# Keys, group-0 values and bias tables of a dilated attention layer sent through DRAM instead of through TensorE

## The chip, the cores and the metric

The kernel runs on one core of a Trainium2 chip. The metric is the device time of one execution in microseconds (us). Five engines share the work: TensorE (PE in the profile, with PEld for its weight loads), VectorE (DVE), ScalarE (ACT), GpSimd (POOL) and SyncE (SP), which here only issues DMAs. Each engine works off its own list of instructions strictly in order, so an instruction that waits holds up everything behind it on its engine.

## The reference, cut to what matters

Two encoder layers over 512 tokens of width 1024, 16 heads of 64 columns, all in float32. Layer A is a dilated attention: one projection gives, for each of three groups (dilations 1, 4, 16), a query, a key and a value, and a gate.

```python
for g, (window, dilation) in enumerate(((128, 1), (512, 4), (2048, 16))):
    q = rms_norm(qkv[:, :, g, 0], q_gain[g])      # per head, over 64 columns
    k = rms_norm(qkv[:, :, g, 1], k_gain[g])
    v = qkv[:, :, g, 2]
    logits = q @ k.T * scale + bias[t5_bucket(rel * dilation)]   # |rel| <= reach, else -1e30
    o, lse = softmax(logits) @ v, log-denominator
y = sum_g softmax_g(lse) * o                       # the three groups merged
x = x + (y * silu(gate)) @ w_out
```

Layer B is a two-dimensional neighbourhood attention of the same size; the change does not touch its code, only the tile that its raw queries and keys live in.

## The kernel before

**Tiling.** Layer A goes through eight chunks `hc`, each of two heads (128 columns). A chunk has these projections on PE: `rawk` (keys of groups 1 and 2, and their values `v12`), `rawq` (queries of the three groups and the key of group 0), `v0_a` (value of group 0, computed transposed) and `gate_a`. Float32 is split into a high and a low part (`wh`, `wl` for the weights, `hn_h`, `hn_l` for the tokens), and three matmuls make one product (`mm3`). Weights come in 512 KB loads `wraw` (three buffers), ACT casts `wh`, and DVE or POOL subtracts for `wl` (four buffers each).

**Order.** PE's order is written out by hand: `main()` yields the projections, `side()` the attention of the chunk before, and `run` slips pieces of the one between pieces of the other by a running estimate of PE's time (`clock`). `later_on(delay, job)` places a job at such a time. On ACT, DVE, POOL and SP the compiler's scheduler chooses the order, except where `tc.keep_in_program_order` holds it. All DMAs but one go through SP's queue.

**Queries and keys.** Scores need queries and keys with the 64 head columns on the partitions, the projection gives tokens on the partitions. In chunks 0 to 5 (`moved(hc)`) the queries and group 0's key are turned without PE: DVE transposes 32x32 blocks in place (`turn_q`, L574), SP writes the tile to DRAM (`qd<-rawq`, L613) and reads it back in another order (`qt<-qd`, L619), and ACT scales group 0's key into `k0` (`split_q`, L638 with L652). The keys of groups 1 and 2 go through PE: `k_a` makes eight 128x128 transposes in each chunk (`transpose4`, L219), DVE scales them into `k12` (L566). The value of group 0 is turned by four PE transposes in `v_a`, and ACT copies them into `v0` (L647). The attention of chunk `hc` runs while PE projects chunk `hc + 1`: `rawk` of `hc + 1`, then `weigh` of chunk `hc - 1` (`PE o`), then the scores of chunk `hc` (`PE log`) between matmuls of `rawq`. Probabilities already go through DRAM as well (`td<-tr`, L764, and `pt<-td`, L768).

**Bias.** `bias_lines` multiplies a one-hot table with the bias table on PE (`pl`), subtracts from a mask on DVE and writes short lines to DRAM. `bias_a` reads them for each chunk into `e0` and `e12` with six loads (`e<-l_d`, L714, L721) whose rows overlap: the source pattern steps back by one row for each partition, and its outermost dimension counts 4.

Of the kernel before, what the change touches and what calls it, by code (L numbers as in the profile page):

```python
# [46 lines left out]
def tile_hybrid_encoder(  # L47
# [6 lines left out]
    t5t: bass.AP,  # L54
    rpb: bass.AP,
    onehot: bass.AP,
# [39 lines left out]
    l0_d = dr.tile([16, 4, 400], F32, name="l0_d")  # L96
    l12_d = dr.tile([16, 512], F32, name="l12_d")
# [186 lines left out]
    def squares(v, ss, i, ns):  # L284
        sq = wk.tile([P, 512], F32, tag="sq", name="sq")[:, : ns * 64]
        if len(v.shape) == 3:
            v = v.rearrange("p (a f) r -> p a f r", f=4)
            nc.gpsimd.tensor_mul(sq.rearrange("p (f a r) -> p a f r", f=4, a=4), v, v)
# [8 lines left out]
    def head_norm(raw, ss, ns, held, delay=0, quick=False):  # L297
# [5 lines left out]
        def scale():  # L303
            for i in range(4):
                by = rs[:, i * ns : (i + 1) * ns].unsqueeze(2)
                if len(raw.shape) == 4:
                    v = raw[:, :, i, :].rearrange("p (h a f) r -> p f h a r", h=2, f=4)
                    by = rs[:, i * ns : (i + 1) * ns].rearrange("p (f h) -> p f h", h=2)
                    by = by.unsqueeze(3).unsqueeze(4).to_broadcast([P, 4, 2, 2, 32])
# [4 lines left out]
                if held or delay:  # L314
                    tc.keep_in_program_order(m)

# [98 lines left out]
    def bias_lines():  # L415

        oh = wk.tile([32, 896], F32, tag="rawq", name="oh", bufs=1)
        tc.keep_in_program_order(nc.sync.dma_start(oh, onehot))
        t5 = cp.tile([32, 48], F32, name="t5")
        nc.sync.dma_start(t5, t5t)  # L420
# [23 lines left out]
    rk = wk.tile([P, 4608], F32, tag="rawk", name="rawk", bufs=1)  # L444
# [6 lines left out]
    def project_qk(n, ns, key, hc, guard, first=False, **kw):  # L451

        box = []

        def evac(i, acc):
            if not box:
                if key == "rawq":
                    t = wk.tile([P, 4 * n], F32, tag="rawq", name=key, bufs=1)
                    box.append(
                        t.rearrange("p (c i r) -> p c i r", c=16, i=4)  # L460
                        if moved(hc)
                        else t.rearrange("p (i c) -> p i c", i=4)
                    )
                elif key == "rawk":
                    box.append(part(0))
                    st["v12", hc] = part(1 + hc % 3)
                elif key == "v":
                    box.append(rk[:, 4 * n * hc : 4 * n * hc + 4 * n].rearrange("p (i c) -> p i c", i=4))
                else:
                    t = wk.tile([P, 4 * n], F32, tag="rawq", name=key, bufs=1)  # L470
                    box.append(t.rearrange("p (i c) -> p i c", i=4))
                box.append(None if key == "v" else wk.tile([P, 32], F32, tag="ss", name="ss"))
            raw, ss = box
            if key == "rawq" and moved(hc):
                src = acc.rearrange("p (f a r) -> p f a r", f=4, a=4)
                pieces = [(raw[:, :, i, :].rearrange("p (a f) r -> p f a r", a=4), src)]
            elif key == "rawk":
                pieces = [(raw[:, i, :], acc[:, :256]), (st["v12", hc][:, i, :], acc[:, 256:])]
            else:
                pieces = [(raw[:, i, :], acc[:, :n])]  # L480
# [5 lines left out]
            if not first and key != "v":  # L486
                squares(raw[:, :, i, :] if key == "rawq" and moved(hc) else raw[:, i, : ns * 64], ss, i, ns)
# [843 lines left out]
```

## Time and profile before

| | |
|---|---|
| time, median of 3 runs | 842.3 us (841.99 to 843.98) |
| the profiled execution: its own time, its span | 842.18 us, 840.4 us |
| PE busy / DVE / ACT / POOL | 833.6 / 515.4 / 425.1 / 283.5 us |
| granted TensorE clock | 1.000 |
| DMA | 141.25 MB, mean 168 GB/s; SP's queue q1 holds 54.6% of 16 engines' span |

The span runs from the first to the last instruction; 1.8 us of the profiled time lie outside it. In rows of the timeline the columns are start, duration, engine, line, operation, output and input tiles, count, and in brackets the idle time before it and what ended it. A matmul's duration (0.39 us) overlaps with the next; the distance of starts (0.227 us) is what PE's time is made of.

### The profile page before, as it was taken

To read this page: it belongs to the slowest core of one execution; us is meant where nothing else is said; L and a number is where in the kernel's file an instruction comes from. 1 tells how busy PE (TensorE), PEld (TensorE's weight loads), DVE (VectorE), ACT (ScalarE), POOL (GpSimd) and SP (SyncE) were. 2 spreads that over 40 slices of the span, in tenths; PEclk is the share of its full clock that TensorE was granted. 3 is DMA by queue.
4 is the path that set the end of the run, shared out by engine and by line. 5 is a ranking of instruction groups with operands and counts; after the bars stand their busy time and mean duration, and the time that the engine had idled before them with its cause. 6 is when DMAs were issued, how large, how long until landed. Compare 5 with 4: busy or idle time off the path is not lost.

```text
span 840.4 us, 15567 instructions
## 1 busy us (share of the span) xinstructions
PE 833.6 (99%) x5698; PEld 675.0 (80%) x5698; DVE 515.4 (61%) x1355; ACT 425.1 (51%) x893; POOL 283.5 (34%) x432
## 2 busy tenths in 40 slices
PE   9999999999999999999999999999999999999998
PEld 7788888788788788788788787888878877777787
DVE  7355684684584675575574755548456778668653
ACT  7432653553552652652653564345375465663551
POOL 3352442441441432432531341112521625235211
PEclk9999999999999999999999999999999999999999
DMA  7346468478368478387376364165236646457223
GB/s 254 112 122 189 150 194 245 164 215 260 127 186 238 143 222 245 107 228 231 111 221 184 111 195 126 56 231 183 78 98 182 180 142 182 129 151 204 102 94 132
DMA packets 64221, 141.25 MB, mean 168 GB/s; under 512 B 5648, under 2 KB 23248, under 8 KB 64144
## 3 DMA queue, kind: packets, MB, share of 16 engines
q1 hardware_dynamic: 64000, 139.99, 54.6%
q8 instruction: 45, 0.74, 0.4%
q14 instruction: 32, 0.26, 0.1%
q10 hardware_dynamic: 144, 0.26, 0.1%
HBM read 109.11 MB, written 31.12 MB: 167 GB/s over the span
## 4 chain that ended last, share of the span: by engine, by line
PE 93%; ACT 3%; DVE 2%; issue 1%; DMA 1%; POOL 0%; SPq 0%; DVEq 0%; ACTq 0%
PE acc L215 79%; PE o L215 5%; PE log L215 5%; PE tp L219 3%; ACT p L1101 1%; ACT p L679 1%; DVE hn_l L403 1%; DMA wraw<-in_w 1%; ACT wh L132 0%; DVE raw L313 0%; DVE p L1091 0%; ACT raw L485 0%; DVE pt L999 0%; DVE wl L138 0%; PE pa L215 0%
## 5 line engine op out<-in xcount | busy, mean ns | idle before, releaser
L132 ACT CAST wh<-wraw 128x512 fp32r<-128x512 f32 (+1 forms) x259 | 158.4, 613 | 288.8 <-PE acc L215 236.7
L215 PE MATMUL acc<-wh,hn_h 128*128 128x512 f32 x704 | 281.9, 401 | 1.3 <-ACT hn_h L402 0.7
L215 PE MATMUL acc<-wl,hn_h 128*128 128x512 f32 x704 | 274.1, 390 | 0.3 <-POOL wl L138 0.3
L215 PE MATMUL acc<-wh,hn_l 128*128 128x512 f32 x704 | 274.3, 390 | 0.0
L138 POOL TENSOR_TENSOR wl<-wraw,wh 128x512 fp32r<-128x512 f32 (+1 forms) x104 | 135.5, 1302 | 362.6 <-ACT wh L132 337.9
L138 DVE TENSOR_TENSOR wl<-wraw,wh 128x512 fp32r<-128x512 f32 (+1 forms) x156 | 114.2, 732 | 148.7 <-ACT wh L132 148.0
L215 PEld LDWEIGHTS acc<-wh,hn_h 128*128 128x128 f32 x704 | 132.1, 188 | 35.5 <-issue 5.6
L215 PEld LDWEIGHTS acc<-wh,hn_l 128*128 128x128 f32 x704 | 132.1, 188 | 28.6
L215 PEld LDWEIGHTS acc<-wl,hn_h 128*128 128x128 f32 x704 | 132.4, 188 | 25.9 <-POOL wl L138 0.8
L215 PE MATMUL acc<-y,wh 128*128 128x512 f32 (+1 forms) x272 | 82.4, 386 | 0.0
L215 PE MATMUL acc<-hn_h,wh 128*128 128x512 f32 x192 | 76.1, 397 | 0.8 <-ACT rawk L485 0.6
L215 PE MATMUL acc<-hn_h,wl 128*128 128x512 f32 x192 | 74.9, 390 | 0.0
L215 PE MATMUL acc<-hn_l,wh 128*128 128x512 f32 x192 | 74.8, 390 | 0.0
L679 ACT ACTIVATE p<-p,mn 128x512 f32<-128x512 f32 (+3 forms) x128 | 69.3, 585 | 0.7 <-DVE mn L678 0.2
L291 DVE TENSOR_REDUCE ss<-sq 128x4 f32<-128x256 f32 (+1 forms) x96 | 48.5, 505 | 28.1 <-POOL sq L290 18.3
L839 ACT ACTIVATE p<-p,mn 128x512 f32<-128x512 f32 (+1 forms) x64 | 44.9, 702 | 38.5 <-DVE mn L828 38.5
L755 DVE STREAM_TRANSPOSE tr<-p 128x512 f32<-128x512 f32 (+1 forms) x80 | 53.6, 684 | 9.3 <-ACT p L679 8.7
L215 PEld LDWEIGHTS acc<-y,wh 128*128 128x128 f32 x272 | 48.3, 189 | 9.6 <-issue 1.3
L215 PE MATMUL acc<-y,wl 128*128 128x512 f32 (+1 forms) x136 | 51.5, 379 | 0.0
L215 PEld LDWEIGHTS acc<-hn_h,wh 128*128 128x128 f32 x192 | 36.0, 188 | 9.2 <-ACT rawk L485 1.0
L215 PEld LDWEIGHTS acc<-hn_h,wl 128*128 128x128 f32 x192 | 36.0, 188 | 7.7
L215 PEld LDWEIGHTS acc<-hn_l,wh 128*128 128x128 f32 x192 | 36.1, 188 | 7.1
(128 smaller groups left out, 965.6 us busy)
## 6 DMA issues: line engine op xcount, KB each, us to landing
wraw<-in_w SPq DMA_DIRECT2D x119, 512.0 KB
td<-tr SPq DMA_DIRECT2D x14, 1024.0 KB
pt<-td SPq DMA_DIRECT2D x56, 256.0 KB
qd<-rawq SPq DMA_DIRECT2D x6, 1024.0 KB
qt<-qd SPq DMA_DIRECT2D x24, 256.0 KB
td<-tr SPq DMA_DIRECT2D x6, 896.0 KB
pt<-td SPq DMA_DIRECT2D x24, 224.0 KB
e<-l_d SPq DMA_DIRECT2D x32, 112.0 KB
```

Source lines behind the costliest of these rows:

```text
L132: nc.scalar.copy(h, raw)
L138: eng.tensor_sub(l, raw, h.bitcast(F32))
L215: nc.tensor.matmul(o, l, r, **kw)
L219: nc.tensor.transpose(o, i, ident)
L291: nc.vector.tensor_reduce(ss[:, i * ns : (i + 1) * ns], sq.rearrange("p (a b) -> p a b", b=64), axis=AX.X, op=ALU.add)
L403: return nc.vector.scalar_tensor_tensor(l, xk, g, h.bitcast(F32), op0=ALU.mult, op1=ALU.subtract)
L679: nc.scalar.activation(pr, pr, AF.Copy, scale=mn[:, 3:4])
L755: nc.vector.transpose(dst, src[:, :n].rearrange("p (i b k) -> p i b k", b=4, k=32))
L839: nc.scalar.activation(row, row, AF.Exp, bias=mn[:, 1:2], scale=-1.0, accum_out=mn[:, 2:3])
L1101: nc.scalar.activation(pr[:, o : o + n], pr[:, o : o + n], AF.Exp, bias=mn[:, 0:1], scale=-1.0, accum_out=mn[:, 2:3])
```

## The change

In chunks 0 to 5 the keys of groups 1 and 2 no longer pass through PE. They are evacuated into the same tile as the queries (`rq`, 3072 columns in place of 2048; blocks 4 and 5 of each group of six), turned there by DVE (`turn_raw`), written and read together with the queries (rows of 768 elements, 1.5 MB in place of 1 MB each way), and scaled in place by ACT after they land. Scores read them from `qt`. In chunks 0 to 6 group 0's value is turned by one DVE transpose, a 256 KB write and four 64 KB reads, and ACT's copy into `v0` reads the result. The bias lines are subtracted once from a table that is now laid out on the host, written to DRAM (`line_d`), and copied by six DMAs from DRAM to DRAM into shifted rows; a chunk's bias then takes one load of 128 rows and four of 32. The raw key and value tile `rk` shrinks by 512 columns, since keys left it.

```diff
     def head_norm(raw, ss, ns, held, delay=0, quick=False, then=None):
...
+            if then:
+                then()
...
-        for g, (o, n) in enumerate(((0, 384), (384, 256), (640, 256))):
-            pl = bank("pl")
-            matmul(pl[0:16, :n], t5[:, 16 * g : 16 * g + 16], oh[:, o : o + n], start=True, stop=True)
-            nc.vector.tensor_sub(mk[:, o : o + n], mk[:, o : o + n], pl[0:16, :n])
-        for j in range(4):
-            nc.sync.dma_start(l0_d[:, j, j : j + 384], mk[:, 0:384])
-        nc.sync.dma_start(l12_d, mk[:, 384:896])
+        nc.vector.tensor_sub(mk, mk, t5)
+        nc.sync.dma_start(line_d, mk)
...
+        jobs = [(l0_d[:, 32 * j : 32 * j + 32, :], shifted(127 - j, 4, 256)) for j in range(4)]
+        jobs += [(l12_d[:, :, 224 * g : 224 * g + 224], shifted(384 + 256 * g + 31, 1, 224)) for g in range(2)]
+        for n, job in enumerate(jobs):
+            later_on(3000 + 2500 * n, partial(spread_out, *job))
...
     def normed(raw, ss, ns, key, hc):
-        head_norm(raw, ss, ns, False, 9000 if key == "rawk" and 0 < hc < NHC - 1 else 0)
-        if key == "rawq" and moved(hc):
-            turn_q(raw)
+        delay = (31000 if moved(hc) else 9000) if key == "rawk" and 0 < hc < NHC - 1 else 0
+        head_norm(raw, ss, ns, False, delay, then=partial(turn_raw, key) if moved(hc) else None)
...
+    def turn_raw(key):
+        f0, f1 = FS[key]
+        for a in range(0, 4, 2):
+            x = by_a[:, a : a + 2, P * f0 : P * f1]
+            tc.keep_in_program_order(nc.vector.transpose(x, x))
...
-        vt = wk.tile([P, EXT], F32, tag="vt", name="vt", bufs=1)
-        nc.vector.tensor_mul(trj(vt[:, 64:EXT]), to_trj(acc[0]), trj(rs_trj))
-        nc.gpsimd.tensor_copy(vt[:, 0:64], vt[:, EXT - 64 : EXT])
+        vt = wk.tile([P, S], F32, tag="vt", name="vt", bufs=1)
+        rows = lambda t, a, b: t.rearrange("p (s j) -> p s j", j=4)[:, a:b]
+        for a, b, to in ((0, 112, 16), (112, P, 0)):
+            src = to_trj(acc[0])[:, a:b]
+            nc.vector.tensor_mul(rows(vt, to, to + b - a), src, rows(rs_trj, a, b))
+        if hc < NHC - 1:
+            move_v(hc, vt)
...
+    def move_v(hc, vt):
+        d = dr.tile([4, P, P], F32, name="vd", tag="vd", bufs=2)
+        vx = wk.tile([P, 4, 4, 32], F32, tag="vx", name="vx", bufs=1)
+        nc.vector.transpose(vx.rearrange("p b i r -> p i b r"), vt.rearrange("p (i b r) -> p i b r", i=4, b=4))
...
+        later_on(2500, write)
+        for b in (0, 2, 1, 3):
+            later_on(7000, partial(read, b))
+        later_on(12500, place)
...
-            project_qk(512, 4, "rawk", hc, ("k12", hc - 1), first=hc == 0, need=None if hc else "na"),
+            project_qk(512, 4, "rawk", hc, ("k12" if hc == NHC - 1 else "q", hc - 1), first=hc == 0, need=None if hc else "na"),
...
     def k_a(hc):
-        yield "wait", ("rawk", hc), 12500 if hc == 0 else 22500 if hc < NHC - 1 else 10500
+        if moved(hc):
+            return
...
         def write():
-            src = raw.rearrange("p (a f) i r -> p a (f i r)", f=4)
-            tc.keep_in_program_order(nc.sync.dma_start(d.rearrange("a p x -> p a x"), src))
+            tc.keep_in_program_order(nc.sync.dma_start(d.rearrange("a p x -> p a x"), by_a))
...
         tc.keep_in_program_order(scaled(dst, src, 0))
+        for g in range(2):
+            x = qt[:, :, 4 + g, :]
+            tc.keep_in_program_order(scaled(x, x, g + 1))
...
     def v_a(hc):
+        if hc < NHC - 1:
+            return
...
+        load(e0, l0_d[hs].rearrange("h p c -> p h c"))
+        for j in range(4):
+            dst = e12[32 * j : 32 * j + 32].rearrange("p (h g) c -> p h (g c)", h=2)
+            load(dst, l12_d[hs].rearrange("h r c -> r h c"))
...
-                    (1 + g, j, slice(256 + P * g, 384 + P * g), k12[:, g, :], slice(P * j, P * j + P))
+                    (1 + g, j, slice(256 + P * g, 384 + P * g), qt[:, :, 4 + g, 32 * j : 32 * j + 32])
```

The order on SP shifts in every chunk. This is SP's queue before, from the second probability write of one chunk to the query reads of the next (`td`, `pt`: probabilities; `qd`, `qt`: queries; `wraw`: weights):

```order
L764 DMA td<-tr 128x4x512
L768 DMA pt<-td 32x4x512 x2
L184 DMA wraw<-in_w 128x1024 x2
L768 DMA pt<-td 32x4x512 x2
L184 DMA wraw<-in_w 128x1024 x2
L613 DMA qd<-rawq 128x4x512
L184 DMA wraw<-in_w 128x1024
L619 DMA qt<-qd 32x4x512 x4
```

The same place after the change, from the probability write to the query write (`vx`, `vd`, `vt`: group 0's value; `e`: bias):

```order
L803 DMA td<-tr 128x4x512
L184 DMA wraw<-in_w 128x1024 x2
L807 DMA pt<-td 32x4x512
L574 DMA vd<-vx 128x4x128
L760 DMA e_2698<-l_d 128x2x256
L760 DMA e_2699<-l_d 32x2x448 x4
L807 DMA pt<-td 32x4x512
L578 DMA vt<-vd 32x4x128 x4
L807 DMA pt<-td 32x4x512
L184 DMA wraw<-in_w 128x1024
L807 DMA pt<-td 32x4x512
```

Two weight loads moved ahead of the first probability read, and ten small DMAs (value and bias) came in behind it. Before, the bias loads of this chunk stood ahead of the `td` write.

On DVE, in the same stretch, before: from the scaling of the keys that PE turned to the start of the queries' norm (`ss`: sums of squares, `nv`: the norm).

```order
L566 TENSOR_SCALAR k_3272<-tp,gk 128x512
L755 STREAM_TRANSPOSE tr<-p 128x4x4x32 x2
L566 TENSOR_SCALAR k_3272<-tp,gk 128x512
L138 TENSOR_TENSOR wl<-wraw,wh 128x512
L291 TENSOR_REDUCE ss<-sq 128x8 x3
```

After, the same place, up to the turn of group 0's value:

```order
L794 STREAM_TRANSPOSE tr<-p 128x4x4x32 x2
L138 TENSOR_TENSOR wl<-wraw,wh 128x512
L290 TENSOR_REDUCE ss<-sq 128x8 x3
L138 TENSOR_TENSOR wl<-wraw,wh 128x512
L313 TENSOR_TENSOR rawq<-rawq,rs 128x2x4x32 x4
L290 TENSOR_REDUCE ss<-sq 128x8
L561 TENSOR_TENSOR vt<-acc,rs_trj 128x448
L561 TENSOR_TENSOR vt<-acc,rs_trj 128x64
L530 STREAM_TRANSPOSE rawq<-rawq 128x2x256 x2
L138 TENSOR_TENSOR wl<-wraw,wh 128x512
L112 TENSOR_SCALAR nv<-ss 128x32
L571 STREAM_TRANSPOSE vx<-vt 128x4x4x32
```

The two key scalings from PE's output are gone; the norm of the keys (four multiplications), their turn and the value's turn now stand here, ahead of the queries' norm.

More of the change, by code (lines that the diff above doesn't have):

```diff
@@ L560, in k_a @@
     def k_a(hc):
-        yield "wait", ("rawk", hc), 12500 if hc == 0 else 22500 if hc < NHC - 1 else 10500
-        k12 = wk.tile([P, 2, 512], F32, tag="k12", name="k12", bufs=1)
+        if moved(hc):
+            return
+        yield "wait", ("rawk", hc), 22500 if hc < NHC - 1 else 10500
+        qt = q_tiles(hc)[0]
         raw = st.pop(("rawk", hc))
@@ L628, in land @@
             assert not left[0]
[L629 to L630 removed]
+            split_q(qt, k0)
             yield
@@ L794, in scores @@
                 ]
-                for g, j, cols, keys, of in parts:
+                for g, j, cols, keys in parts:
                     for hd in range(2):
```

167 lines of the change are left out of this document (84 added, 83 removed).

## Prediction

> **What bounds the kernel now.** I read the page first, then who waits for whom, then the chain in order of time. The page:
>
> ```profile
> span 840.4 us, 15567 instructions
> PE 833.6 (99%) x5698; PEld 675.0 (80%) x5698; DVE 515.4 (61%) x1355; ACT 425.1 (51%) x893; POOL 283.5 (34%) x432
> PE 93%; ACT 3%; DVE 2%; issue 1%; DMA 1%; POOL 0%; SPq 0%; DVEq 0%; ACTq 0%
> ```
>
> PE is busy for 99% of the span and 93% of the chain that ended last is its own. The list of PE's waits begins with:
>
> ```profile
> PE busy L377 <- DVE warm L366: 0.9, 1, 0.9
> PE acc L215 <- ACT hn_h L402: 0.7, 1, 0.7
> ```
>
> Nothing made PE wait longer than 0.9 us, and both rows belong to the start or to the change of layers. So in layer A a PE instruction that goes away shortens the span, as long as nothing becomes late enough to make PE wait. The chain around the attention of chunk 4, and its one piece with `pl`:
>
> ```profile
> 300.29 0.44 PE tp L219 x4
> 302.12 0.44 PE tp L219 x4
> 325.73 0.44 PE tp L219 x4
> 341.18 3.62 PE o L215 x48
> 346.39 1.84 PE log L215 x96
> 36.82 1.61 PE pl L215 x6
> ```
>
> Four transposes hold the chain for 0.44 us (two groups for the keys, one for the value), and the one-hot products for 1.61 us.
>
> **What goes.** Chunks 0 to 5 lose two groups each, chunks 0 to 6 one: 12 + 7 = 19 groups, 19 x 0.44 = 8.4 us. The products with the one-hot table go once: 1.6 us. Together 10.0 us, all on the path. How one transpose reads by itself:
>
> ```profile
> L219 PE MATMUL tp<-ident,rawk 128*128 128x128 f32 x64 | 9.6, 272 | 0.0
> L215 PE MATMUL o<-pt,rawk 128*64 128x128 f32 x320 | 22.4, 278 | 0.0
> ```
>
> 272 ns is its duration with the overlap; a quarter of 0.44 us, 110 ns, is what it adds. The Trainium skill (TensorE: Matmul & The Clock Gate, Part 4: PE-mode transpose) gives about 275 ns for one in a kernel: by that the 76 transposes would be worth an estimated 20.9 us, against 8.4 us by the chain. The durations agree, but as a price the measured distance decides.
>
> The scores now read those keys in runs of 32 columns out of `qt`. The second row has a moving operand in runs of 32 too and takes 278 ns against 272, so I add nothing (bound: 6 ns on 8 chunks x 4 tiles x 2 groups x 4 residues x 2 heads = 512 matmuls, 3.1 us if none of it overlapped).
>
> **What is added off PE, and its cover.** The long new chain is: turn on DVE, write `qd`, read `qt`, scale on ACT, scores. Here it is for chunk 3 and chunk 4, from the timelines of SP, ACT and PE:
>
> ```profile
> 264.68 0.43 SPq L613 DMA_DIRECT2D qd<-rawq  x1
> 271.34 1.75 SPq L619 DMA_DIRECT2D qt<-qd  x4
> 273.22 3.03 ACT L485 ACTIVATE rawk<-acc,rs_n 128x256 f32<-128x256 f32 x8
> 277.77 1.20 ACT L652 ACTIVATE k<-qt,gk 128x512 f32<-128x512 f32 x1 [1.02 <-DMA qt<-qd]
> 282.40 1.86 PE L215 MATMUL log<-k,qt 64*32 64x192 f32 x93
> ...
> 322.11 1.29 DVE L574 STREAM_TRANSPOSE rawq<-rawq 128x512 f32<-128x512 f32 x2
> 325.10 0.43 SPq L613 DMA_DIRECT2D qd<-rawq  x1
> 332.35 1.75 SPq L619 DMA_DIRECT2D qt<-qd  x4
> 337.14 3.03 ACT L485 ACTIVATE rawk<-acc,rs_n 128x256 f32<-128x256 f32 x8
> 340.51 1.29 ACT L652 ACTIVATE k<-qt,gk 128x512 f32<-128x512 f32 x1
> ```
>
> In chunk 3 ACT waited for the read, which landed 277.77 - 271.34 = 6.4 us after its issue; in chunk 4 it did not wait. With 6.4 us there too, the read landed at 338.8, and the scaling could have ended 346.39 - 338.8 - 1.29 = 6.3 us ahead of the scores. That is the cover. Against it stand:
>
> ```profile
> 336.00:338.00 2.00, 2.00 (x10) 1.65 (x9) 0.69 (x1) 1.48 (x4) 0.31 (x1) 1.00 1.08 249
> 357.00:359.00 2.00, 2.00 (x62) 1.45 (x68) 0.94 (x3) 0.00 (x0) 0.00 (x0) 1.00 1.02 395
> L679 ACT ACTIVATE p<-p,mn 128x512 f32<-128x512 f32 (+3 forms) x128 | 69.3, 585 | 0.7 <-DVE mn L678 0.2
> ```
>
> The last two columns of the stretches are the busy share of 16 DMA engines and GB/s. While a write like `qd` and a weight load run, 395 GB/s move; while query reads and a weight load run, 249. So the write's extra 0.5 MB costs 1.3 us and the read's 2.1 us (at the least nothing, if rows of 3 KB in place of 2 KB carry it; at the most half of the whole, 3.6 us of the write's 7.25 and 3.2 us of the read's 6.4). I take the rates, since these stretches run full. Two more scalings on ACT: 1.2 us. The scores come 0.44 us earlier, by the value's transposes. Sum 5.0 of 6.3 us: 1.3 us are left.
>
> DVE comes in ahead of it. Its new work in front of the queries' turn:
>
> ```profile
> L313 DVE TENSOR_TENSOR rawk<-rawk,rs x32: 382/415/1489, 46.6 to 505.5; 128x256 f32<-128x256 f32 x32
> L574 DVE STREAM_TRANSPOSE rawq<-rawq x24: 662/699/705, 66.6 to 386.7; 128x512 f32<-128x512 f32 x24
> 239.13 1.37 DVE L566 TENSOR_SCALAR k<-tp,gk 128x512 f32<-128x512 f32 x2
> ```
>
> Four multiplications 1.7, the keys' turn 1.4, the value's turn 0.7, the second piece of `vt` 0.2 (an estimate from the first), less 1.4 for the two scalings that went: 2.6 us. Chunk 4's turn ended at 323.4 and its write went out at 325.10, so 1.7 us of that are covered and the write goes out 0.9 us later. Left: 0.4 us. With spread from chunk to chunk I charge 0.2 us in each of chunks 1 to 5, 1.0 us (bounds: 0 and, by the rivals below, 18). Chunk 0 costs nothing; its scaling came 13 us after the read's issue:
>
> ```profile
> 75.66 3.03 SPq L619 DMA_DIRECT2D qt<-qd  x4
> 88.65 1.31 ACT L652 ACTIVATE k<-qt,gk 128x512 f32<-128x512 f32 x1
> ```
>
> The bias loads speak for the cover. The stretch in which they run alone, SP's waits for the probability write, and what follows from them in chunk 3:
>
> ```profile
> 302.00:304.00 2.00, 2.00 (x12) 1.71 (x11) 1.61 (x3) 1.46 (x4) 1.30 (x1) 1.00 0.27 91
> SPq L768 <- DMA td<-tr: 69.2, 14, 10.9
> 261.00 0.62 ACT L132 CAST wh<-wraw 128x512 fp32r<-128x512 f32 x1 [6.78 <-DMA wraw<-in_w]
> ```
>
> They keep 0.27 of the engines, about 4 of 16, at 91 GB/s; their pattern's outermost dimension counts 4. A `td` write that needs all 16 queues behind them, SP stands up to 10.9 us on it, and weights come late (ACT stood 6.8 us, and still PE did not). `td` and `qt`, with 128 and 32 outermost, fill the engines. The new loads have 128 and 32, so 0.7 MB should take some 2.8 us at 249 GB/s. The Trainium skill (DMA: Bandwidth & Descriptors, Rules for kernel authors) says the same of an outermost dimension under 16: it confines a DMA to as many engines. The row agrees; that the new shapes get all 16 no row here shows.
>
> The rest has cover and costs nothing. `weigh` needs the value at 341.18, and its transposes stood 15 us ahead of that, time enough for a 256 KB write and reads at the rates above; if they are late, ACT's copy holds the casts behind it, and chunk 3 shows 6.8 us of such a hold without a wait on PE. Evacuations write the same number of elements in runs of 32. The six copies inside DRAM move 3 MB, at 249 GB/s 12 us of DMA time spread over 15, once; without cover late weights cost at most those few us once. POOL loses its copy of `vt`. Layer B's order is the same on every engine.
>
> Sum: 842.2 (the profiled execution, 0.1 under the median of 842.3) - 8.4 - 1.6 + 1.0 = **833.2 us**.
>
> **Rivals.** *DVE late (gain cut, 836 to 839.7).* The 1.7 us of cover on DVE count only if SP is free: the weight load ahead of `qd` waits for a `wl` that DVE now makes behind the queries' turn. Then the full 2.6 us reach the scores, 1.7 more than charged less the 0.4 left: 1.3 us in five chunks, 6.5 us, 838.7. For it: the 0.4 us margin; against: the shorter `td` waits.
>
> *DMA paced by backlog (slower).* If the write and the read grow by half in their whole issue-to-landing times, 3.6 + 3.2 instead of 1.3 + 2.1, the read lands 3.4 us later than charged. Place: ACT's first scaling, before the scores of chunks 1 to 5; ACT stands there and PE behind it. Price: 3.4 + 0.2 in five chunks, 18 us: 832.2 + 18 = 850. It decides against the change from 2.0 us a chunk, where 10 us are gone. For it: chunk 3, where only 3.4 us lay between the end of the scaling and the scores, and the keys' evacuation (273.22) began 1.9 us after the write had landed; that evacuation now goes into the very tile that the write reads, so a late write also holds PE's banks. Against: chunk 3's write was late through the weights above.
>
> The Trainium skill (VectorE: DVE Perf Modes, Rules for kernel authors) has 128x128 transposes go to TensorE. By that rule the change moves the wrong way; here PE is the full engine, and the rule would be borne out only by these two rivals.
>
> *Nothing moves (839.7 to 844.8).* A loss of 1.5 to 2.5 us a chunk cancels the gain. That PE's time does not shrink at all is unlikely: no engine feeds it late.
>
> **How the numbers follow.** Forecast (831 to 836) 0.52; below 831 0.02, if the slower matmuls after each group go too; DVE late 0.23; cancelled 0.08; slower 0.15. A measurement of this kernel can tell about 0.3%, 2.5 us, from no change, so faster is below 839.7: 0.52 + 0.02 + 0.23 = 0.77, same 0.08, slower 0.15. The range of 831 to 843 leaves out 0.02 below and, above, 0.15 and the upper third of the cancelled case, 0.03.
>
> **What would show it.** Right: 19 pieces `tp` and the piece `pl` gone from the chain, PE's waits for `k<-qt` or `qt` under 1 us a chunk, ACT's wait ahead of L697 (the new line of the scaling) short or nil, the `td` waits on SP shorter, bias stretches above a share of 0.27. Wrong: PE's waits ahead of `log` or ahead of `rawq`'s first matmuls of 2 us or more in each of chunks 1 to 5, or weights that PE waits for.

## The result, and the profile after

| | before | after |
|---|---|---|
| time, median of 20 runs each | 842.25 us (841.88 to 844.24) | 844.12 us (840.3 to 846.4) |
| ratio | | 1.0009, 95% interval 0.9998 to 1.002 |
| the profiled execution: its own time, its span | 842.18 us, 840.4 us | 845.74 us, 844.0 us |
| granted TensorE clock | 1.000 | 0.995 |
| DMA | 141.25 MB | 154.08 MB |

No change that a measurement can tell; the forecast was 833.2 us. The profiled execution is one of the slowest of its kernel, so what it lost is more than what the median lost. The page after, its head and the chain that ended last:

```profile
span 844.0 us, 15462 instructions
PE 831.6 (99%) x5616; PEld 669.3 (79%) x5616; DVE 516.2 (61%) x1356; ACT 430.4 (51%) x905; POOL 282.2 (33%) x424
PE 72%; DMA 13%; DVE 7%; ACT 4%; issue 2%; SPq 1%; POOL 1%; ACTq 0%; DVEq 0%; POOLq 0%
```

82 matmuls have gone (5698 to 5616: 76 transposes and the 6 one-hot products), and "99% busy" still stands there. The chain tells more: PE held 93% of it and now holds 72%; DMA went from 1 to 13%. Who PE waits for:

```profile
PE log L215 <- ACT k L697: 4.5, 4, 2.0
PE acc L215 <- ACT rawk L493: 1.0, 2, 0.6
PE acc L215 <- ACT rawq L493: 0.9, 3, 0.4
PE log L215 <- ACT qt L697: 0.8, 5, 0.2
```

Before, no wait of the scores was in this list. Now they wait for the scaling of group 0's key (`k`), in four places, up to 2.0 us, and in five for the two scalings that were added (`qt`). The chain that the prediction followed, in chunk 4 after the change, from the timelines of SP and ACT:

```profile
331.99 0.43 SPq L654 DMA_DIRECT2D qd<-rawq  x1
340.37 1.74 SPq L660 DMA_DIRECT2D qt<-qd  x4
349.25 1.22 ACT L697 ACTIVATE k<-qt,gk 128x512 f32<-128x512 f32 x1 [4.69 <-DMA qt<-qd]
350.38 1.32 ACT L697 ACTIVATE qt<-qt,gk 128x512 f32<-128x512 f32 x2
```

From the write's issue to the read's 8.4 us (before 7.25), from the read's issue to the first scaling 8.9 us (before 6.4, chunk 3), and ACT stands idle for 4.7 us until the read lands. For most of that stretch the DMA engines are full (last two columns of the stretches: share of 16 engines, GB/s), first with the write, then with the read:

```profile
332.00:334.00 2.00, 2.00 (x10) 1.69 (x9) 0.69 (x1) 0.82 (x2) 1.05 (x1) 1.00 1.06 249
344.00:346.00 2.00, 2.00 (x23) 1.56 (x23) 1.13 (x3) 0.57 (x2) 1.29 (x4) 1.00 1.05 221
```

Where the wait is longest, in chunk 1, PE's timeline and the stretches (third number from the end: granted clock) read:

```profile
155.83 0.66 PE L215 MATMUL log<-k,qt 64*32 64x192 f32 x16 [1.98 <-ACT k L697]
157.06 0.68 PE L215 MATMUL log<-qt 64*32 64x128 f32 x16 [0.16 <-ACT qt L697]
158.34 1.10 PE L215 MATMUL log<-qt 64*32 64x128 f32 x32
159.37 0.79 PE L215 MATMUL acc<-wh,hn_h 128*128 128x512 f32 x1
```

```profile
156.00:158.00 2.00, 1.84 (x64) 1.04 (x70) 0.17 (x1) 2.00 (x4) 0.41 (x1) 0.73 0.08 23
158.00:160.00 2.00, 2.00 (x50) 1.31 (x35) 1.58 (x10) 1.61 (x4) 2.00 (x2) 0.50 0.00 0
160.00:162.00 2.00, 2.00 (x10) 1.65 (x9) 2.00 (x11) 2.00 (x6) 0.39 (x1) 0.92 0.03 8
```

PE waits 1.98 us, then the scores take 3.54 us (155.83 to 159.37) where they took 1.84, because each group of keys is scaled while PE stands inside the scores, and because PE's clock is granted at 0.73 and 0.50 just there. The same happened in chunk 3 (1.81 us of wait, 0.66 and 0.50 behind it); in chunks 2, 4 and 5 the waits were 0.6 us or less and the clock stayed at 1.00.

A chunk's scores come in two pieces, here called the first and the second scores (`u` 0 and 1 in the code). To see what each chunk loses I take PE's timeline and measure from the first matmul of `o` (values of the chunk before) to the first of the second scores. Without a wait that is 16.8 us in every chunk.

| start of `o` to second scores, us | chunk 1 | 2 | 3 | 4 | 5 | over 16.8, sum |
|---|---|---|---|---|---|---|
| before | 16.8 | 16.8 | 16.8 | 16.8 | 16.8 | 0 |
| after | 21.0 | 17.6 | 20.8 | 17.8 | 18.0 | 11.1 |

That is the gain, given back: 11.1 us in the five places. They split in three. PE waits 4.9 us ahead of the first scores (2.0, 0.1, 1.9, 0.3 and 0.6). The first scores last 0.7 us longer in each chunk, 3.4 us, as the scalings come one by one. And the slower clock costs 1.4 us in chunk 1 and in chunk 3, 2.8 us. Two more terms complete the profiled time: the stretch from chunk 0's second scores to the next `o` takes 47.0 us in place of 46.4, though two groups of four transposes and the value's (1.3 us) left it, 1.9 us lost (in early_scores, with the same code there, it takes 45.5, so not every execution loses this); and this execution's start was about 2 us slow (last section). 842.2 - 10.0 + 11.1 + 1.9 + 2 = 847.2, against 845.74 measured. Of the 1.5 us between them some 0.9 belong to the 10.0, as is shown further on; the rest is not placed.

### The profile page after: what moved, and what is told of

Read it like the earlier page. It is cut to its first block, busy times and chain, and to the rows that moved or that the text cites. A ratio compares the mean times of both kernels' runs of the same rounds, so it can differ in the third digit from the quotient of the medians.

```text
span 844.0 us, 15462 instructions
## 1 busy us (share of the span) xinstructions
PE 831.6 (99%) x5616; PEld 669.3 (79%) x5616; DVE 516.2 (61%) x1356; ACT 430.4 (51%) x905; POOL 282.2 (33%) x424
## 2 busy tenths in 40 slices
DMA packets 73324, 154.08 MB, mean 183 GB/s; under 512 B 6640, under 2 KB 32368, under 8 KB 73248
## 4 chain that ended last, share of the span: by engine, by line
PE 72%; DMA 13%; DVE 7%; ACT 4%; issue 2%; SPq 1%; POOL 1%; ACTq 0%; DVEq 0%; POOLq 0%
PE acc L215 62%; DMA qt<-qd 5%; PE log L215 4%; DMA qd<-rawq 4%; PE o L215 3%; PE tp L219 2%; DMA e<-l_d 2%; DVE rawq L313 2%; DVE rawq L530 1%; DVE wl L138 1%; ACT p L1140 1%; DMA wraw<-in_w 1%; ACT p L724 1%; ACT qt L697 1%; DMA td<-tr 1%
## 5 line engine op out<-in xcount | busy, mean ns | idle before, releaser
L313 DVE TENSOR_TENSOR rawq<-rawq,rs 128x256 f32<-128x256 f32 (+1 forms) x96 | 55.0, 632 | 4.1 <-POOL rs L124 3.7
L287 POOL TENSOR_TENSOR sq<-rawq 128x256 f32<-128x256 f32 (+1 forms) x48 | 42.6, 900 | 17.6 <-ACT rawq L493 15.9
L493 ACT ACTIVATE rawq<-acc,rs_n 128x512 f32<-128x512 f32 (+1 forms) x76 | 44.9, 611 | 2.8 <-DMA qd<-rawq 2.5
```

What stands on the lines that cost most here:

```text
L287: nc.gpsimd.tensor_mul(sq.rearrange("p (f a r) -> p a f r", a=4, r=32), v, v)
L313: m = nc.vector.tensor_mul(v, v, by)
L493: nc.scalar.activation(dst, src, AF.Copy, scale=rs_n[:, i : i + 1])
```

## The experiments

The theory after the result, A: PE's 10 us are real, and are lost again at the scores of chunks 1 to 5, which wait for the q/k chain. Rivals: B, the values' move holds the weights; C, the DVE alone is late; and that the transfers' length alone does it. Ratios are to the kernel before on the same chip, with 95% intervals.

**late_scores.** The scores later in PE's order, to give the cover back.

```diff
-    yield "wait", ("rawk", hc + 1), 5200 if u == 0 else 16800 if hc else 14200
+    yield "wait", ("rawk", hc + 1), (8500 if hc else 5200) if u == 0 else 19000 if hc else 14200
```

> Edit: in chunks 1 to 5 the first scores stand 3.3 us later in PE's order (8500 for 5200) and the second 2.2 us later (19000 for 16800); nothing else. Theory A (PE waits at the scores for the read of qt and the two added ACT scalings, and its clock drops behind each wait of about 2 us): the waits of PE log on k, rawk and qt (4.5 + 1.0 + 0.8 us) and the drops in chunks 1 and 3 go, 8 us or more, 834 to 837 us. Rival B (late weights and ACT held behind the value copy cost the time, the scores only show it): the waits move on to the next place, 841 to 845 us. Rival C (the DVE is late): as A here.

Measured 851.7 us, 1.0103 (1.0086 to 1.0119): slower, as neither said. PE's waits:

```profile
PE acc L215 <- ACT rawq L493: 9.3, 8, 5.5
PE log L215 <- ACT k L697: 0.3, 1, 0.3
```

The wait of the scores did go, 4.5 to 0.3 us. But the second scores, moved along, put their softmax on ACT just where ACT evacuates `rawq`, and PE's banks wait 9.3 us for that. The experiment changed two things; late_first below changes one.

**no_key_gain.** The two added ACT scalings left out.

```diff
-        for g in range(2):
-            x = qt[:, :, 4 + g, :]
-            tc.keep_in_program_order(scaled(x, x, g + 1))
```

> Leaves out the two ACT scalings with which the gains are put on the landed keys of groups 1 and 2 (chunks 0 to 5); the scores then depend on the read and on the scaling of group 0's key alone. Theory A with the scalings as the larger part: 1.3 us a chunk in chunks 1 to 5 and the drops of clock that need a wait of about 2 us, 5 to 9 us less, 835 to 839 us. Rival: the read alone is late; the wait for it stays, 2 to 4 us less, 840 to 842 us.

839.0 us, 0.9958 (0.9944 to 0.9972). That is 4 us (by the ratios) to 5 us (by the medians) under the changed kernel, at the edge of theory A's range: the scalings stand on the path, with 0.6 us a chunk inside the first scores (2.0 us long in place of 2.6), and this profiled execution has no clock drop. Their 1.3 us on ACT are not paid whole. The waits for `k` remain (5.9 us in five places), so they are not all of it.

**early_turn.** The DVE's work for the keys moved away from the queries' turn.

```diff
-        delay = (31000 if moved(hc) else 9000) if key == "rawk" and 0 < hc < NHC - 1 else 0
+        delay = (11000 if moved(hc) else 9000) if key == "rawk" and 0 < hc < NHC - 1 else 0
```

> Edit: norm and turn of the keys of groups 1 and 2 in chunks 1 to 5 come 11 us after their projection in the order, not 31 us, so that the DVE has only the queries' norm and turn and the value's in front of the write of qd. Rival C (DVE late is what makes the scores wait): the write goes out about 3 us earlier as before the change, 836 to 839 us. Theory A without C (the write and the read themselves are longer and the scalings serial): the write goes out earlier but the read lands less than 1.5 us earlier, 841 to 844 us.

842.4 us, 0.9995 (0.998 to 1.0009), outside rival C's 836 to 839. The write of `qd` did go out earlier, 15.6 us ahead of `o` in chunk 4 in place of 13.0. But from the write's issue to the read's 9.7 us passed in place of 8.4, and from there to the first scaling 9.4 in place of 8.9. Issued earlier, the write runs behind the reads of values and probabilities, in stretches whose engines are at a share of 0.87 to 1.04 (324 to 334 us); two thirds of what the DVE gave back, the DMA took. That, and not the time alone, speaks against C, for the edit also brought a wait of its own: in chunk 0's stretch PE waits 2.0 us at once for `rawq` (111.3 to 113.3 us). In the five places the profiled execution loses 6.5 us in place of 11.1, 3.8 of them in chunk 1.

**values_by_pe.** The whole change without its value part.

```diff
     def v_a(hc):
-        if hc < NHC - 1:
-            return
         yield "wait", ("vt", hc), 2500
```

(`v0_a` makes `vt` as before the change.)

> Group 0's value turned by PE again in all chunks, as before; keys and bias as after the change. PE gets 7 groups of 4 transposes back, 3.1 us. Theory A: the traffic and the DVE work of the values are a small part of what is late; 845 to 848 us. Rival B (the value's write, reads and the ACT copy that waits for them hold the weights up): 837 to 841 us.

839.1 us, 0.9961 (0.9942 to 0.998): faster than the change by 4 us (ratios) to 5 us (medians), though PE has 3.1 us more to do, where theory A expected 845 to 848. So the value part costs 7 to 8 us here, by rival B's numbers. Its mechanism is not borne out: no weight kept PE waiting in the changed kernel beyond 0.2 us in all. What differs in the profiles is that the write of `qd` goes out 0.9 us earlier (13.9 us ahead of `o` in chunk 4, for 13.0), and that the clock stays at 1.00. The five places lose 7.7 us in place of 11.1, and 2.8 of these 3.4 us are the clock. The rest of the 7 to 8 us is not placed, and this profiled execution (843.85 us) is the slowest of its ten.

**bias_only, bias_and_values.** The parts of the change put on the kernel before, first the bias part, then the value part too.

```diff
     def v_a(hc):
+        if hc < NHC - 1:
+            return
         yield "wait", ("vt", hc), 2500
```

(That is bias_and_values over bias_only, with `move_v` and `v0_a` as after the change; bias_only has `bias_lines`, `bias_a` and the host's table as after the change, and nothing else.)

> The kernel before with the bias part of the change alone (no one-hot products on PE, shifted rows in DRAM, one load of 128 rows and four of 32 a chunk). By the prediction's terms: 1.6 us of PE go and nothing else is on the path, 840 to 841 us. Rival: the six copies inside DRAM delay weights in chunk 0, no change or slower, 842 to 845 us.

> The kernel before with the bias part and the value part of the change; keys still by PE. PE loses 1.6 + 3.1 us. The scores do not read the values; if the value part costs time in the changed kernel only because its turn delays the write of qd, then here, where the scores have 3 to 6 us of cover, it is a gain: 836 to 838 us. If the move of the values costs by itself (ACT held by the copy that waits for the reads, late weights, more traffic): 840 to 844 us.

840.1 us, 0.9976 (0.9966 to 0.9986), and 836.5 us, 0.993 (0.9916 to 0.9945). The bias part gives 1.9 us for 1.6 of `pl`, the value part another 3.6 for 28 transposes, 3.1 us by the chain's 110 ns each (by the 272 ns that one lasts it would have been 7.6 us). So moving the values costs nothing by itself, with all its five DMAs a chunk and ACT's waits ahead of the copy (25.7 us in six places, up to 4.9). No chunk loses anything: 16.8 us in all five. The same value part that gains 3.6 us here costs 4 to 5 with the keys' part. An explanation that fits, but was not tested by itself: the some 1 us a chunk by which it makes the write of `qd` later falls on a chain that has 3.3 us or more of cover here and none there. Chunk 4 of bias_and_values, SP and ACT, with the first scores at 341.9:

```profile
330.67 1.75 SPq L649 DMA_DIRECT2D qt<-qd  x4
337.22 1.21 ACT L684 ACTIVATE k<-qt,gk 128x512 f32<-128x512 f32 x1 [0.93 <-DMA qt<-qd]
```

**longer_rows.** The transfers' length by itself.

```diff
-    wk.tile([P, 4, 4, P], F32, tag="q12", name="qt", bufs=1)
+    wk.tile([P, 4, 6, P], F32, tag="q12", name="qt", bufs=1)
-    d = dr.tile([4, P, 512], F32, name="qd", tag="qd", bufs=2)
+    d = dr.tile([4, P, 768], F32, name="qd", tag="qd", bufs=2)
-    src = raw.rearrange("p (a f) i r -> p a (f i r)", f=4)
+    src = sb(raw.rearrange("p c i r -> p (c i r)"), 0, [[424, 4], [1, 768]])
```

> The kernel with the bias and value parts (836.5), keys by PE, but the write of qd and the reads of qt carry rows of 768 elements (1.5 MB each way) as in the changed kernel; the rows overlap in the source, so the queries that arrive are other columns, and only the time is to be read. No DVE or ACT work is added. By the changed kernel's times the chain from the write's issue to the landing grows by about 4 us, and the cover in that kernel is 3.4 to 4.5 us: waits of PE log on k of 0 to 1 us a chunk, 836.5 to 840 us. Rival (the transfers' length alone takes the gain): 842 us or more. Rival (the length is harmless, the DVE and ACT work is the cause): 836 to 837 us, ACT ready as early as before.

839.25 us, 0.9949 (0.993 to 0.9968). The same place in chunk 4:

```profile
333.44 1.75 SPq L649 DMA_DIRECT2D qt<-qd  x4
342.45 1.23 ACT L684 ACTIVATE k<-qt,gk 128x512 f32<-128x512 f32 x1 [3.60 <-DMA qt<-qd]
```

The read takes 9.0 us from its issue where 1 MB took 6.55; the write 9.95 us where it took 9.3. That uses up the cover and loses 0.8 and 1.0 us in chunks 1 and 5, nothing in the others (16.8): 1.8 us, against 1.6 us by the ratios (2.75 by the medians). Longer transfers are a part of the loss, not the loss: the write here goes out 13.7 to 16.1 us ahead of `o`, in the changed kernel 11.5 to 13.2.

**late_first, pe_values_late_first, pe_values_early_turn.** Only the first scores of chunks 1 to 5 2.0 us later (7200 for 5200), on the changed kernel and on the one with the values by PE; and the early turn on the latter.

```diff
-    yield "wait", ("rawk", hc + 1), 5200 if u == 0 else 16800 if hc else 14200
+    yield "wait", ("rawk", hc + 1), (7200 if hc else 5200) if u == 0 else 16800 if hc else 14200
```

> After the change, with only the first scores of chunks 1 to 5 moved by 2.0 us in PE's order (7200 for 5200); the second scores stay. If the second scores' softmax on ACT, run into the evacuation of rawq, was what cost late_scores its time, that wait (9.3 us) is gone here; the waits at the scores shrink by up to 2 us a chunk and so does the number of clock drops: 836 to 840 us. Rival (any later score pushes the softmax into the evacuation): PE acc on ACT rawq waits again, 845 us or more.

> Values by PE as in the run before (839.1), and the first scores of chunks 1 to 5 moved by 2.0 us in PE's order. If the waits at the scores (3.9 us on k, 0.8 on qt, and 0.7 us a chunk inside the scores) are what is left to lose: 833 to 836 us. If they only move to the evacuation of rawq: 838 to 842 us.

> Values by PE as in the run before (839.1), and norm and turn of the keys 11 us after their projection in place of 31. If the DVE sets when the write of qd goes out, that goes out 2 to 3 us earlier and the waits of PE log on k (3.9 us) fall under 1 us: 834 to 837 us. If the read's landing is set by the DMA backlog instead, 838 to 840 us.

840.2 us, 0.9982 (0.9958 to 1.0006); 837.7 us, 0.9944 (0.9929 to 0.9959); 838.75 us, 0.9969 (0.9952 to 0.9986). The first is 2 us (ratios) to 4 us (medians) under the changed kernel, but the intervals overlap, and the wait for `rawq` is 0.9 us in place of 9.3. That points to the second scores for what late_scores lost, though its first scores also stood 1.3 us later than here. The second kernel missed its range by 1.7 us though its score waits fell to 0.7 us. It still loses 2.2 us between `o` and the second scores. The third missed 834 to 837 as well and lies in the range given for a landing that the DMA backlog sets, but not for that reason: the scores hardly wait (0.5 us), but on DVE the keys' norm and turn in chunk 1 now stand ahead of a softmax, and PE waits 2.1 us for `rawq` once.

**early_scores.** The waits made longer, to see whether they are paid at their length and whether the clock follows them.

```diff
+    yield "wait", ("rawk", hc + 1), (3200 if hc else 5200) if u == 0 else 16800 if hc else 14200
```

> After the change, with the first scores of chunks 1 to 5 moved 2.0 us earlier in PE's order (3200 for 5200). The keys land when they land, so each wait at the scores grows by about 2 us, to 2 to 4 us. If a wait costs its own length and is partly given back by the work that then stands behind it: near 844 us as after, since the same work is done between the same landings; 5 waits of 2 us more, 853 us, if it is not given back. If waits from about 2 us up also pull the granted clock down in every one of the five chunks (1.5 to 1.7 us each, now in two): 4 to 5 us on top, 856 to 859 us, and a mean clock under 0.99.

844.1 us, 1.0021 (1.0007 to 1.0035). The landing sets the time and the work passed over is done behind it: the sum over 16.8 is 10.9 us, near the 11.1 after the change, of which 2.8 were the clock. The second half of the expectation fell. The longest wait ahead of scores in any profile here, and the clock behind it:

```profile
154.34 0.66 PE L215 MATMUL log<-k,qt 64*32 64x192 f32 x16 [2.33 <-ACT k L697]
156.00:158.00 2.00, 2.00 (x56) 1.58 (x38) 1.47 (x9) 1.86 (x5) 1.90 (x2) 1.00 0.00 0
```

The clock stayed at 1.00 here and through this whole execution, so a wait of 2 us does not by itself bring a drop (the last section shows what does). Seven of the other nine executions of this kernel have a mean clock of 0.996 or 0.998.

**after_both_shifts, pe_values_both_shifts.** Early turn in chunks 2 to 5 and late first scores together, with the values moved and with the values by PE.

```diff
-        delay = (31000 if moved(hc) else 9000) if key == "rawk" and 0 < hc < NHC - 1 else 0
+        delay = (11000 if hc > 1 else 31000 if moved(hc) else 9000) if key == "rawk" and 0 < hc < NHC - 1 else 0
```

(and the line of late_first)

> After the change, whole, with norm and turn of the keys early (11 us) in chunks 2 to 5 and the first scores of chunks 1 to 5 2.0 us later. If waits of the scores for the q/k chain are what took the gain, both shifts together give the cover back in chunks 2 to 5 and most of the 10 us come out: 834 to 836 us. If the value part costs time elsewhere: 838 to 840 us, not below the kernel with the values by PE and the late scores (837.7).

> Same two shifts with the values by PE. The waits at the scores were already 0.7 us in all with the late scores alone, so little is left to gain: 835.5 to 837.5 us.

839.8 us, 0.9963 (0.9938 to 0.9988), and 836.35 us, 0.9934 (0.9918 to 0.995). Shifting alone does not save the whole change: in chunk 4 the write then takes 11.3 us to the read's issue. This is what it runs in:

```profile
322.00:324.00 2.00, 2.00 (x11) 1.65 (x10) 0.00 (x0) 0.00 (x0) 0.00 (x0) 1.00 1.00 193
```

Full engines at 193 GB/s, half of the 395 of the write's stretch in the prediction: the last reads of values and probabilities still run there, on 32 partitions each.

**keys_apart.** All work of the change, but the keys out of the queries' chain: in chunks 2 to 5 they go to DRAM and back on their own, at a time when the DMA engines have room (a share of 0.49 and 0.55 from 300 to 304 us, where the reads for chunk 4 go out), and ACT scales them over 30 us ahead of the scores.

```diff
+    def send_keys(hc):
+        turn_raw("rawk")
+        d = dr.tile([4, P, 256], F32, name="kd", tag="kd", bufs=2)
...
+        later_on(7000, write)
+        for a in (0, 2, 1, 3):
+            later_on(13000, partial(read, a))
+        later_on(20000, lambda: key_gains(q_tiles(hc)[0]))
```

> The whole change, but in chunks 2 to 5 the keys of groups 1 and 2 leave on their own: norm and turn 11 us after their projection, a write of 0.5 MB 7 us behind that, four reads and the two ACT scalings long ahead of the scores; the queries' write and read are 1 MB as before the change. If the gain was lost in the queries' chain (longer transfers, two scalings at its end, DVE work at its start), the waits of PE log in chunks 2 to 5 go and only chunk 1 loses its 2 to 4 us: 832.5 to 836 us, below all kernels so far. If total DMA traffic in the chunk sets the landing, the chain stays late: 839 to 843 us.

836.2 us, 0.9921 (0.9896 to 0.9946). PE's waits of the scores, from chunk 1 alone:

```profile
PE log L215 <- ACT k L723: 2.2, 1, 2.2
PE log L215 <- ACT qt L723: 0.2, 1, 0.2
```

Chunks 2 to 5 are back at 16.8 us each; chunk 1, still as in the change, has 20.8. The median missed the range by 0.2 us.

**keys_apart_all, keys_apart_all2.** Chunk 1's keys too, at two places.

```diff
-    apart = lambda hc: moved(hc) and hc > 1
+    apart = lambda hc: moved(hc) and hc > 0
...
+        t = (5000, 10000, 16000) if hc == 1 else (7000, 13000, 20000)
```

(write, reads and scalings; norm and turn of chunk 1 at 20000. In keys_apart_all2 they stand at 26000, and the three at 1000, 5500 and 11000.)

> As keys_apart, and chunk 1's keys leave on their own too (norm and turn 20 us after their projection, behind the second softmax of chunk 0; write 5 us later). If the whole gain hangs on the queries' chain, chunk 1's two score intervals go back to 16.8 us in sum (20.8 in keys_apart's profile) and the time to 842.2 - 10.0 = 832 us, 831.5 to 834. If the keys' DVE work or transfers come in the way of the queries' norm in chunk 1: 834 to 837 us.

> The same with chunk 1's norm and turn 26 us after its projection and the write 1 us later, closer to the queries' own. Same expectation, 831.5 to 834 us; if the two writes now stand behind each other and the query write is late again, 834 to 837 us.

834.9 us, 0.9923 (0.9907 to 0.994), and 842.8 us, 1.0008 (0.9998 to 1.0019). In the first all five chunks stand at 16.8 to 17.0 us, and its profiled execution took 832.85 us, within 1 us of the 832.2 that the 10 us promise. Its median is above its range by 0.9 us. Each has one wait in the stretch ahead of chunk 1's scores, where the keys' work now stands in the way of something else. The first of these rows is of keys_apart_all, the second of keys_apart_all2:

```profile
PE acc L215 <- ACT rawq L493: 2.6, 3, 2.2
```

```profile
PE o L215 <- DMA pt<-td: 8.0, 1, 8.0
```

The second placement made probabilities land 8 us late, once; that and the clock drop behind it (a mean of 0.994) cost the gain. The lowest median of all is keys_apart_all's; its interval overlaps that of bias_and_values (836.5) and of keys_apart, so it is shown to beat the kernel before and the change, not those two.

| start of `o` to second scores, us | chunk 1 | 2 | 3 | 4 | 5 | over 16.8, sum |
|---|---|---|---|---|---|---|
| early_scores | 19.9 | 17.7 | 19.5 | 19.1 | 18.7 | 10.9 |
| after_both_shifts | 19.0 | 18.9 | 18.1 | 18.3 | 17.7 | 8.0 |
| values_by_pe | 19.3 | 18.9 | 17.9 | 17.5 | 18.1 | 7.7 |
| no_key_gain | 18.6 | 17.6 | 18.2 | 17.4 | 18.8 | 6.7 |
| early_turn | 20.6 | 16.8 | 18.0 | 17.0 | 18.0 | 6.5 |
| pe_values_late_first | 18.0 | 16.8 | 17.5 | 16.8 | 17.2 | 2.2 |
| longer_rows | 17.6 | 16.8 | 16.8 | 16.8 | 17.8 | 1.8 |
| keys_apart | 20.8 | 16.8 | 16.8 | 16.8 | 16.8 | 4.0 |
| keys_apart_all | 17.0 | 16.8 | 16.8 | 16.8 | 16.8 | 0.2 |

## Why the prediction was wrong

**What goes, 10.0 us: right, and a little small.** bias_only and bias_and_values show 5.5 us for 4.7 predicted of these parts. keys_apart_all's profiled execution, the fastest of its four, is 9.3 us under before's with 2.6 us of waits for `rawq` still in it. From one `o` to the next PE takes 63.9 us before, 63.4 in bias_and_values, where one group of four transposes a chunk is gone, and 62.5 in keys_apart_all, where three are: 0.5 us a group, charged 0.44, or 0.9 us more over the 19 groups. So a transpose is worth some 120 ns and not its 272. By the 275 ns of the Trainium skill (TensorE: Matmul & The Clock Gate, Part 4: PE-mode transpose), taken as a price, the value part would have promised an estimated 7.7 us, twice what it gave.

**The transfers' price: close.** Over chunks 1 to 5 the write took 8.5 us from its issue to the read's (7.5 before), the read 8.9 to 9.4 us to ACT (6.4 before): +1.0 and about +2.8, charged 1.3 and 2.1.

**DVE's lateness, 0.9 us: the step that failed.** The prediction set 2.6 us of new work on DVE against 1.7 us of cover on SP, between the end of the turn and the write. That cover was not there. On SP a weight load stands ahead of the write, and it waits for a `wl` that DVE makes behind the turn. It was so in chunk 4 before the change, where the turn ends at 323.4:

```profile
323.33 0.71 DVE L672 SCALAR_TENSOR_TENSOR gt<-eg,gt 128x256 f32<-128x256 f32 x2
323.96 0.68 DVE L138 TENSOR_TENSOR wl<-wraw,wh 128x512 fp32r<-128x512 f32 x1
324.70 0.35 SPq L184 DMA_DIRECT2D wraw<-in_w  x1
325.10 0.43 SPq L613 DMA_DIRECT2D qd<-rawq  x1
```

It is so after the change, where the chain that ended last runs through all of it, from the turn to the landing (its main pieces):

```profile
328.67 2.28 DVE rawq L530 x2
330.95 0.59 DVE wl L138
331.59 0.36 SPq L184
331.99 8.30 DMA qd<-rawq
341.68 7.46 DMA qt<-qd
```

A later turn makes a later `wl`, and with it a later write. In chunk 4 the turn ended 3.7 us later and the write went out 13.0 us ahead of `o` in place of 16.0, 3.0 us late; only the `gt` that now stands ahead of the turn was saved. Chunks 2, 3 and 5 show the same order. In chunk 1, where the write goes out 11.5 us ahead of `o`, SP waits 1.6 us just ahead of it for a weight load to land. The lateness begins ahead of the queries' norm: its first row on DVE stands 25.6 us ahead of `o`, before 28.4. Over chunks 1 to 5 the write goes out 16.0 to 16.3 us ahead of `o` in bias_only, which has the new bias loads and none of the new DVE work, and 11.5 to 13.2 after the change: 3.3 us later in the mean, where 0.9 and the 0.44 of the value's transposes were charged.

**The cover, 6.3 us in every chunk.** It was worked out for chunk 4, and there it held: 6.3 less 3.0 for the later write, 1.1 and 2.5 for the longer transfers is -0.3, and PE waited 0.3 us. To use it for all five chunks had no ground in the rows of before. ACT's waits show 3.4 us in chunk 3, which the prediction quoted, and 4.3 in chunk 1; in chunks 2, 4 and 5 no wait shows the landing, and a read of 6.4 us gives an estimated 5.8, 6.3 and 5.4. What made up for it is the change's own bias part: in bias_only the writes of chunks 1 and 3 go out 16.3 and 16.0 us ahead of `o` in place of 13.4 and 12.5, and the same estimate gives 6.5, 5.8, 6.6, 7.5 and 5.1, 6.3 in the mean. The prediction had said that the bias loads speak for the cover, but it did not count this; that chunk 4's figure fits the mean is luck. From there the chain closes: 3.3 for the later write, 1.2 for the longer one (against bias_only's 7.3) and 2.8 for the read are 7.3 us, 1.0 more than the cover, and PE waits 4.9 us in five chunks.

**What was not in the sum.** The two scalings were charged 1.2 us against the cover. But they run one after the other while PE stands inside the scores, and with the cover used up that costs PE 0.7 us in every chunk, 3.4 us. The clock dropped in two chunks of the profiled execution, 2.8 us. Chunk 0's stretch lost 1.9 us in it, which I had priced at nothing. That the scores read the keys in runs of 32 columns costs nothing, as charged: in keys_apart_all the first scores of chunks 2 to 5 last 1.91 us, as before.

**The rivals.** "DVE late" named the step that failed, the weight load that waits for `wl` behind the turn, and its 2.6 us. It gave 838.7, since it kept the other terms; early_turn shows that an early turn alone does not bring the gain back, as the DMA takes most of the lead. "Nothing moves" gave 839.7 to 844.8 from a loss of 1.5 to 2.5 us a chunk; 11.1 us over five chunks is 2.2. It was given 0.08, and it named no mechanism of its own. "DMA paced by backlog" is borne out in part: the read grew by 2.8 us of the 3.2 that it gave, the write by 1.0 of 3.6. In early_turn and after_both_shifts the write did grow, to 9.7 and 11.3 us in chunk 4.

**What went as foretold beside it.** SP's waits for the probability write were 69.2 us, up to 10.9:

```profile
SPq L807 <- DMA td<-tr: 27.6, 10, 5.8
SPq L660 <- DMA qd<-rawq: 28.1, 6, 6.6
```

They fell to 27.6, and bias_only has 26.4, so the new bias loads alone do it; but 9 us more went into waiting for the longer `qd` (19.1 before). The signs that the prediction named for being wrong (waits of 2 us or more in each chunk) were too coarse: two waits of about 2 us, three of 0.6 or less, the serial scalings and the clock were enough.

## What to carry to other kernels

A gap between an instruction and the next link of its chain is cover only if nothing in it moves along when the instruction comes later: look what fills the gap, here a `wl` and a weight load that come behind the turn. Cover belongs to a chunk, not to a kernel: take it from the chunk that has least, and where no wait shows the landing, treat it as unknown. Two moves that ride on one chain must be summed against that chain: the value part gained 3.6 us without the keys' part and cost 4 to 5 beside it. And when work is taken off the full engine, send it at a time of its own when the transfer engines have room rather than with a transfer that already ends last: keys_apart moves as many bytes as the change, and in the chunks where it does so (2 to 5) the waits are gone.

## What the runs showed of the hardware

**Clock drops go by windows of 3.41 us, not by the length of a wait.** In the clock records of the traces each drop is a stretch at half clock that lasts 3.41 us, or twice or three times that (6.83 in late_scores, 10.24 in keys_apart_all2). Within one execution the records lie on one grid of that step: after's begin at 10.15, 156.92, 160.34, 286.63 and 290.04 us. Cut along this grid, the wait of 1.98 us in after (first two rows) lies within one window, and the next runs at half clock; the wait of 2.33 us in early_scores (last two rows) is shared by two windows, and the clock stays:

```profile
153.51:156.92 3.41, 1.40 (x34) 0.47 (x32) 0.00 (x0) 2.32 (x4) 0.14 (x1) 1.00 0.76 273
156.92:160.33 3.41, 3.27 (x66) 2.35 (x67) 2.08 (x12) 3.02 (x8) 2.74 (x2) 0.50 0.00 0
149.69:153.10 3.41, 2.32 (x14) 1.25 (x10) 0.69 (x1) 0.00 (x0) 1.53 (x8) 1.00 1.03 263
153.10:156.51 3.41, 2.01 (x86) 1.34 (x90) 0.41 (x3) 3.39 (x5) 0.41 (x1) 1.00 0.39 150
```

In the 18 traces the five windows at full clock in which PE idles 1.90 us or more are all followed by a drop (after chunk 1, early_turn, keys_apart, late_scores, keys_apart_all2). So are the window of 1.81 us in after's chunk 3 and that of 1.58 us in late_first's chunk 5, where the rest of the window is mostly score matmuls. None of the others is, with 1.86 us or less. That the scores count for less than the large matmuls is argued from these two windows alone. The Trainium skill (TensorE: Matmul & The Clock Gate, Part 1: The HAM clock gate) has the clock watched in a free-running window of about 3.4 us, and the traces agree. Its rule there, no idle gaps over about 3.4 us, was not strict enough here. Where a wait falls in the grid differs between executions of one kernel: the changed kernel's runs have mean clocks of 0.995 to 1.000 and spread over 6 us, where the kernel before spreads over 2.4.

**Two kinds of start.** The first row of matmuls in before's profile and in after's:

```profile
5.09 1.18 PE L215 MATMUL acc<-wh,hn_h 128*128 128x512 f32 x4 [0.71 <-ACT hn_h L402]
5.32 2.08 PE L215 MATMUL acc<-wh,hn_h 128*128 128x512 f32 x4 [0.62 <-ACT hn_h L404]
```

Four matmuls take 1.18 us in one and 2.08 in the other, and so on for the first twelve, 2.2 us in sum. The granted clock of the stretches reads 1.00 in both, but only because the trace has no clock record there. Its first record, at full clock, begins at 3.9 us in before and at 10.15 us in after, and that is where the slow matmuls end. It is so in all 18 traces: the first twelve matmuls take 2.8 to 2.9 us where the first record begins by 4.8 us, and 4.3 to 5.1 us where it begins at 8.9 to 10.4 (one lies between, with 3.5 us and 6.6). So the slow start is a clock that is granted later. It does not go with the change: longer_rows, without its key part, started slow; keys_apart_all, with all of it, fast. The runs of the kernel before fall into two bunches, at 842 and 844 us, about as far apart; that the start makes them is not shown.
